# Score products of a differential attention: two low parts over 64 rows each instead of 128 rows padded with zeros

## The chip, the cores and the metric

The kernel runs on one core of one Trainium2 chip. The metric is the device time of one execution in microseconds; before the change it is 729.48 us, the median of three runs (729.27 to 730.88). All arithmetic is to float32 accuracy: a product that needs full accuracy is written as three products of "high" and "low" parts (the high part is the value rounded to the matrix engine's single-pass format, the low part is the rest).

## The reference, cut to what matters

Two layers over 512 positions of width 1024: a Mamba-2 layer (projections, a convolution, a chunked scan, an output projection) and a differential attention layer. The change is in the second. Eight heads each have two maps of 64 features; the scores of each map are softmaxed and the second map is subtracted with a weight:

```python
def attend_block(args):
    qb, blk = args
    ...
    scores = jnp.einsum("bhiqd,bhikd->bhiqk", qb, k).astype(jnp.float32) * scale
    scores = scores - slopes[None, :, None, None, None] * dist
    probs = jax.nn.softmax(jnp.where(allowed, scores, -jnp.inf), axis=-1)
    weights = probs[:, :, 0] - lam * probs[:, :, 1]
    return jnp.einsum("bhqk,bhke->bqhe", weights.astype(v.dtype), v)
```

## The kernel before, in words

TensorE runs a long dense stream of projections (z, g, o for the first layer; v, k, q, t for values, keys, queries and gates, then b and c for the output projection). Between pieces of it, small steps are put in at places that the program counts out: `beside(n)` lets the dense stream advance by n units (a 512-column triple of products is 2 of them), then the next small step is written. In the attention layer TensorE's instructions keep exactly the order in which they are written; VectorE's (DVE) and ScalarE's (ACT) are placed by a scheduler that works from a modelled timeline. Weights are fetched by DMA from SyncE into `raw`, split by ACT (`whi`) and DVE (`wlo`) one piece at a time, and used one stage later.

The small steps of a head h go over four tiles t of 128 queries. `scores(h, t)` makes the scores of both maps of that tile against the first n = (t + 1) * 128 keys; `weigh` and `turn` combine the two maps and transpose the result, `values` multiplies with v, `norm_head` and `gate_head` finish the head. A call of `scores` thus has products of 128, 256, 384 or 512 columns, eight calls of each width, 32 in all. The very last one, head 7 and tile 3, stands near the end, where the final projection (pc) runs out.

How a score is made: feature f of map m sits on partitions 64m to 64m + 63. The tile k2 (`two` in `feat_proj`) has for map m the high part of k on m's own 64 partitions and the low part on the other 64; q2 has the high part of q on both. One product over all 128 rows is therefore q_high times (k_high + k_low). The second product adds q_low times k_high: `q_lo` has, for map m, the low part of q on m's own 64 partitions and zeros on the other 64, so that k's low part is multiplied by nothing. These zeros are written once, by four memsets on GpSimd (POOL, line 897); DVE writes the low parts of each head into the other half (`q_lo<-pq,q` in the profile).

The products of one call stand in the order map 0 high, map 0 low, map 1 high, map 1 low, each pair into a bank of PSUM of its own (`ss_bank`, shown as sc). DVE then takes each map's bank with one instruction that scales, adds the distance penalty and finds the minimum (in the profile CUSTOM_DVE_ANT_0 s<-sc,bias), and ACT makes the exponentials and their sum (ACTIVATE s<-s,mx). The banks go round: three of the kind ss, and every fourth take is one of the four of the dense stream.

One other place uses part of the array: pyd in the scan of the first layer, whose products have 64 output columns and alternate between the upper and the lower half of the output partitions.

Nearly all instructions come through one helper, so the profile shows them at line 55; they are told apart by the tiles they write and read. PE is TensorE's products, PEld its loads of the stationary operand.

Of the kernel before, what the change touches and what calls it, by code (L numbers as in the profile page):

```python
# [9 lines left out]
F32 = mybir.dt.float32  # L10
F32R = mybir.dt.float32r
# [6 lines left out]
P = 128  # L18
S = 512
# [44 lines left out]
def trunk(ctx, tc, x, x_t, par, w_dt, w_in, w_out, w_kvqg, w_bo, d_skip, lam_qk, fin_g, out):  # L64
    nc = tc.nc
    V, A, T = (Ordered(tc, e) for e in (nc.vector, nc.scalar, nc.tensor))
    GP = nc.gpsimd
# [7 lines left out]
    def mm_bank(name):  # L75
        return psum.tile([P, 512], F32, tag="mm", name=name, bufs=4)
# [4 lines left out]
    def ss_bank(name):  # L81
        turns[0] += 1
        tag = "mm" if turns[0] % turns[1] >= 3 else "ss"
        return psum.tile([P, 512], F32, tag=tag, name=name, bufs=3 if tag == "ss" else 4)

    def long_bank(name):
        return psum.tile([P, 512], F32, tag="long", name=name)
# [118 lines left out]
    def use_b(seg, first=None, pace=None):  # L206
        i = segs.index(seg)
        while pieces:
            lay(pieces.pop(0))
        if i + 2 < len(segs) and fetched[0] == i + 2:  # L210
            loaded[i + 2] = load(i + 2)
        if seg == ("o", 3, 0):
            for piece in loaded.pop(i + 2)():
                lay(piece)
        if i + 1 in loaded:
            new = loaded.pop(i + 1)()
            pace = pace or 32 // len(new)
            pieces.extend(p + (pace if k else first or pace,) for k, p in enumerate(new))
        return ready.pop(seg)
# [15 lines left out]
    def mm3(ps, lhs, rhs, first, last, **kw):  # L235
        (lh, ll), (rh, rl) = lhs, rhs
        T.matmul(ps, lhsT=lh, rhs=rh, start=first, stop=False, **kw)
        T.matmul(ps, lhsT=lh, rhs=rl, start=False, stop=False, **kw)
        T.matmul(ps, lhsT=ll, rhs=rh, start=False, stop=last, **kw)
# [191 lines left out]
    q2 = sm.tile([P, P], F32, name="q2")  # L431
# [281 lines left out]
    cp = ctx.enter_context(tc.tile_pool(name="cp", bufs=1))  # L713
# [12 lines left out]
                yield 1  # L726
            A.copy(v_sb[:, t, cs], pv[:, 0:256])

    q_lo = [cp.tile([P, 2, S], F32R, name=f"q_lo{i}") for i in range(2)]
    kT, qT, gT, oT = {}, {}, {}, {}  # L730

    def feat_proj(pair):
        wh, wl = use_b((pair[0], pair, 0))
        for i in range(2):
            kind, h = pair[2 * i], int(pair[2 * i + 1])
            pf = mm_bank(f"p{kind}{h}")
            cs = slice(i * P, (i + 1) * P)
            for k in range(KD):
                mm3(pf, (wh[:, k, cs], wl[:, k, cs]), (hh[:, k, :], hl[:, k, :]), k == 0, k == KD - 1)
                yield 2  # L740
            if kind == "t":

                th = small.tile([P, S], F32, tag="wide", name=f"th{h}", bufs=2)
                A.activation(th, pf, AF.Tanh, scale=0.5)
                gt = cp2.tile([P, S], F32, tag="gt", name=f"gt{h}", bufs=3)
                V.scalar_tensor_tensor(out=gt, in0=th, scalar=1.0, in1=pf, op0=ALU.add, op1=ALU.mult)
                gT[h] = gt
            else:

                two = cp2.tile([P, 2, S], F32R, tag=f"{kind}2", name=f"{kind}2_{h}", bufs=4 if kind == "k" else 2)  # L750
                for m in range(2):
                    own, far = slice(64 * m, 64 * m + 64), slice(64 - 64 * m, 128 - 64 * m)
                    A.copy(two[own, m, :], pf[own, :])
                    if kind == "q":
                        A.copy(two[far, m, :], pf[own, :])
                    V.tensor_tensor(out=two[far, m, :] if kind == "k" else q_lo[h % 2][own, m, :], in0=pf[own, :],
                                    in1=two[own, m, :].bitcast(F32), op=ALU.subtract)
                (kT if kind == "k" else qT)[h] = two
            done.add(f"{kind}{h}")
# [18 lines left out]
    def stream_b():  # L778
        for it in ORDER_B:
            if it[0] == "c":  # L780
                yield from rows()
                return
            yield from b_out(int(it[1])) if it[0] == "b" else v_proj(int(it[1])) if it[0] == "v" else feat_proj(it)
            done.add(it)
# [3 lines left out]
    def scores(h, t):  # L788

        if t == 0:  # L790
            bias = cp2.tile([P, S], F32, tag="bias", name=f"bias{h}")
            V.tensor_scalar(out=bias, in0=dist, scalar1=-(2.0 ** (2 - h)), scalar2=None, op0=ALU.mult)
            st[h] = (bias, small.tile([P, 2, NT], F32, tag="mx", name=f"mx{h}"),
                     small.tile([P, 2, NT], F32, tag="sums", name=f"sums{h}"), [],
                     small.tile([P, NT], F32, tag="ratio", name=f"ratio{h}"), long_bank(f"po{h}"), [],
                     cp2.tile([P, NT, P], F32, tag="on", name=f"on{h}", bufs=2),
                     small.tile([P, NT], F32, tag="o_ss", name=f"o_ss{h}"))
        bias, mx, sums, s = st[h][0:4]
        k2, q2, ql = kT[h], qT[h], q_lo[h % 2]
        n = (t + 1) * P  # L800
        tq = slice(t * P, (t + 1) * P)
        s.append([cp2.tile([P, S], F32, tag=f"s{i}", name=f"s{h}_{t}_{i}", bufs=2) for i in range(2)])
        for i in range(2):
            ps = ss_bank(f"sc{h}_{t}_{i}")
            T.matmul(ps[:, :n], lhsT=q2[:, i, tq], rhs=k2[:, i, :n], start=True, stop=False)
            T.matmul(ps[:, :n], lhsT=ql[:, i, tq], rhs=k2[:, i, :n], start=False, stop=True)
            so = s[t][i][:, :n]
            V.tensor_tensor_reduce(out=so, in0=ps[:, :n], in1=bias[:, S - n:], scale=-0.125, scalar=3e38,
                                   op0=ALU.add, op1=ALU.min, accum_out=mx[:, i, t:t + 1])
            A.activation(so, so, AF.Exp, scale=-1.0, bias=mx[:, i, t:t + 1], accum_out=sums[:, i, t:t + 1])  # L810
# [81 lines left out]
    V.tensor_copy(dist, disti)  # L892
    A.activation(dist, dist, AF.Abs)
    GP.memset(dist[0:64, S - 64:S], BIG)
    for i in range(2):
        for m in range(2):
            GP.memset(q_lo[i][64 - 64 * m:128 - 64 * m, m, :].bitcast(F32), 0.0)
    lq = cp2.tile([P, 4, 64], F32, tag="gt", name="lq", bufs=3)
    nc.sync.dma_start(lq.rearrange("p a d -> p (a d)"), lam_qk.rearrange("a d -> (a d)").partition_broadcast(P))
    lqv = lq.rearrange("p (a b) d -> p a b d", b=2)  # L900
# [38 lines left out]
    def half(t, n):  # L939
        hs = slice(n * 512, (n + 1) * 512)  # L940
        return x_tok[:, t, hs], fg[:, hs], ot[t][:, hs], out[t * P:(t + 1) * P, hs]
# [40 lines left out]
    for h in range(DH):  # L982
        for t in range(NT):
            share = (13.0, 15.3, 17.6, 19.35)[t]
            if (h, t) == (DH - 1, 2):
                break
            scores(h, t)
            beside(share / 3)
            if h > 1 and t == 0:
                gate_head(h - 2)  # L990
            if last:
                turn(*last)
            beside(share * 2 / 3)
            if last:
                values(*last)
                if t == 0:
                    norm_head(h - 1)
            last = h, t


    h = DH - 1
    turns[:] = [0, 1]
    fg = res.tile([P, D], F32, tag="hT_lo", name="fg")
    nc.sync.dma_start(fg[:], fin_g.partition_broadcast(P))
    scores(h, 2)
    beside(6)
    gate_head(h - 1)
# [3 lines left out]
    norm_head(h, 0, 2)  # L1011
    beside(7.6)
    scores(h, 3)
    ot += [cp2.tile([P, D], F32, tag="k2", name=f"ot{t}", bufs=4) for t in range(NT)]
    beside(2)
# [45 lines left out]
    y, f, o, dst = half(3, 0)  # L1061
# [71 lines left out]
```

## Time and profile before

| | |
|---|---|
| median of three runs | 729.48 us (729.27 to 730.88) |
| profiled execution, its own time | 729.15 us |
| its span, first to last instruction | 727.0 us |
| busy TensorE products / loads | 713.5 / 593.1 us |
| busy VectorE / ScalarE / GpSimd | 528.0 / 433.7 / 117.7 us |
| TensorE share of the chain that ended last | 90% |
| first and last score product begin | 478.8 / 701.9 us |
| score products with q's high part, x64 | 223 to 481 ns each in the record |
| score products with q's low part, x64 | 273 to 398 ns each in the record |

A product's recorded duration runs from its issue to the modelled end of its results; neighbours overlap. What a product costs TensorE is read from the distance between the starts of neighbours. A row of the timeline gives start, duration (of all that were merged into it), engine, line, operation, output<-inputs, shape, and how many instructions. In a product's shape the first part is rows * columns of the array, the second the moving operand. A row of the chain of waits gives start, duration, engine, tile, and how many pieces were merged.

### The profile page before, as it was taken

Reading aid. Unit: us, or ns where it says so; the run is one execution under the profiler, and the core shown is the slowest. Engines: PE = TensorE matmul, PEld = TensorE weight load, DVE = VectorE, ACT = ScalarE, POOL = GpSimd, SP = SyncE. Lnnn points to the kernel's source line nnn. Section 1 sums busy time; section 2 is a strip of 40 time slices with the busy share of each in tenths; the row PEclk is TensorE's granted clock in tenths of the full one; section 3 lists DMA queues with packets and bytes.
Section 4 is the critical chain, followed back from the end, with each engine's and each line's share of the span. In section 5 each row is a group of like instructions: output and inputs, shape, how many; then the busy total and the mean of one; then the engine's idle time right before and its main releaser. Section 6 shows DMA issues by size and latency. Waiting matters only on the chain.

```text
span 727.0 us, 10819 instructions
## 1 busy us (share of the span) xinstructions
PE 713.5 (98%) x3989; PEld 593.1 (82%) x3989; DVE 528.0 (73%) x1202; ACT 433.7 (60%) x965; POOL 117.7 (16%) x158
## 2 busy tenths in 40 slices
PE   9999999999999999999999999999999999999996
PEld 7787888888888888887788869888988898889874
DVE  4688964979479668569995846657667857785886
ACT  5948573654735527527534348667766756756566
POOL 0108241412315024150110101000000000000002
PEclk9999999999999999999999999999999999999999
DMA  8634313314133231231122310331221131122003
GB/s 302 233 131 162 116 59 117 117 58 175 58 117 116 95 137 60 91 142 59 59 70 105 116 59 9 117 115 59 94 82 58 59 117 59 59 90 85 29 1 115
DMA packets 12916, 70.86 MB, mean 97 GB/s; under 512 B 1728, under 2 KB 2496, under 8 KB 5312
## 3 DMA queue, kind: packets, MB, share of 16 engines
q1 hardware_dynamic: 12576, 69.90, 26.5%
q8 instruction: 31, 0.51, 0.3%
q10 hardware_dynamic: 288, 0.28, 0.1%
q14 instruction: 21, 0.17, 0.1%
HBM read 68.02 MB, written 2.16 MB: 97 GB/s over the span
## 4 chain that ended last, share of the span: by engine, by line
PE 90%; DVE 7%; ACT 1%; issue 1%; POOL 0%; ACTq 0%; DVEq 0%; POOLq 0%
PE pg L55 21%; PE po L55 14%; PE pz L55 12%; PE pt L55 7%; PE pv L55 6%; PE pq L55 6%; PE pk L55 6%; PE pb L55 3%; PE sc L55 3%; PE pyd L55 2%; PE pc L55 2%; DVE wlo L55 2%; DVE xc L55 2%; PE pyt L55 1%; PE pxt L55 1%; PE psA L55 1%
## 5 line engine op out<-in xcount | busy, mean ns | idle before, releaser
L55 DVE SCALAR_TENSOR_TENSOR wlo<-raw,prm,whi 128x512 fp32r<-128x512 f32 (+1 forms) x256 | 150.4, 633 | 52.7 <-ACT whi L55 51.3
L55 ACT ACTIVATE whi<-raw,prm 128x512 fp32r<-128x512 f32 (+1 forms) x256 | 136.8, 606 | 81.4 <-PE pg L55 30.1
L55 PE MATMUL pg<-a_hi,whi 128*128 128x512 f32 x256 | 103.3, 404 | 1.5 <-DVE y_c L55 1.5
L55 PE MATMUL pg<-a_hi,wlo 128*128 128x512 f32 x256 | 102.3, 402 | 0.0
L55 PE MATMUL pg<-a_lo,whi 128*128 128x512 f32 x256 | 102.3, 400 | 0.0
L55 DVE SCALAR_TENSOR_TENSOR xc<-pg,prc,xc 128x511 f32<-128x511 f32 (+2 forms) x96 | 69.6, 738 | 4.8 <-ACT xc L55 4.4
L55 PEld LDWEIGHTS pg<-a_hi,whi 128*128 128x128 f32 x256 | 48.1, 188 | 13.1 <-issue 1.9
L55 PEld LDWEIGHTS pg<-a_hi,wlo 128*128 128x128 f32 x256 | 48.1, 188 | 11.0
L55 PEld LDWEIGHTS pg<-a_lo,whi 128*128 128x128 f32 x256 | 48.1, 188 | 10.7
L55 PE MATMUL po<-whi,yh 128*128 128x512 f32 x128 | 51.4, 402 | 1.5 <-DVE xc L55 0.8
L55 PE MATMUL po<-wlo,yh 128*128 128x512 f32 x128 | 51.1, 399 | 0.0
L55 PE MATMUL po<-whi,yl 128*128 128x512 f32 x128 | 50.4, 398 | 0.0
L55 PE MATMUL pz<-wlo,a_hi 128*128 128x512 f32 x128 | 50.3, 399 | 0.0
L55 PE MATMUL pz<-whi,a_lo 128*128 128x512 f32 x128 | 49.8, 398 | 0.0
L55 PE MATMUL pz<-whi,a_hi 128*128 128x512 f32 x128 | 49.6, 401 | 0.0
L971 POOL TENSOR_TENSOR ot<-ot,fg 128x512 f32<-128x512 f32 x4 | 5.1, 1289 | 256.9 <-ACT ot L55 256.9
L55 ACT ACTIVATE s<-s,mx 128x128 f32<-128x128 f32 (+3 forms) x64 | 35.5, 556 | 9.6 <-DVE mx L55 9.1
L55 ACT ACTIVATE xc<-pg,prc 128x512 f32<-128x512 f32 x32 | 24.6, 773 | 26.6 <-DVE pg L55 26.5
L589 POOL TENSOR_TENSOR xe<-xdt,tok 128x256 f32<-128x256 f32 x24 | 17.3, 749 | 139.6 <-DVE xdt L55 139.6
L55 DVE CUSTOM_DVE_ANT_0 s<-sc,bias 128x128 f32<-128x128 f32 (+3 forms) x64 | 29.4, 488 | 12.2 <-PE sc L55 11.7
L55 ACT ACTIVATE xc<-xc 128x512 f32<-128x512 f32 x32 | 20.0, 629 | 28.3 <-DVE xc L55 28.2
L55 PE MATMUL pv<-whi,b_hi 128*128 128x256 f32 x128 | 36.6, 286 | 0.0
(243 smaller groups left out, 1719.7 us busy)
## 6 DMA issues: line engine op xcount, KB each, us to landing
raw<-in_w_in SPq DMA_DIRECT2D x23, 1024.0 KB, 4.8
raw<-in_w_kvqg SPq DMA_DIRECT2D x16, 1024.0 KB, 4.8
dec<-acs_d SPq DMA_DIRECT2D x8, 1024.0 KB, 4.8
raw<-in_w_out SPq DMA_DIRECT2D x8, 1024.0 KB, 4.8
raw<-in_w_bo SPq DMA_DIRECT2D x4, 1024.0 KB, 4.8
x_tok<-in_x SPq DMA_DIRECT2D x4, 512.0 KB, 9.3
out<-ot SPq DMA_DIRECT2D x7, 256.0 KB, 2.4
raw<-in_w_in SPq DMA_DIRECT2D x4, 256.0 KB, 5.8
```

The costliest lines, as they stand in the source:

```text
L55: i = op(*args, **kw)
L589: GP.tensor_tensor(out=xe[:, c], in0=xdt[:, c], in1=toe_tok[:, c, hs].unsqueeze(2).to_broadcast([P, R, HD]), op=ALU.mult)
L971: GP.tensor_tensor(out=o, in0=o, in1=f, op=ALU.mult)
```

## The change

The low parts' tile is half as large and without zeros, the four memsets are gone, and the low products read only the map's own 64 partitions of both operands. Both banks of a call are taken first; the order of the four products is now map 0 high, map 1 high, map 0 low, map 1 low. What DVE and ACT do per map is the same.

```diff
-    q_lo = [cp.tile([P, 2, S], F32R, name=f"q_lo{i}") for i in range(2)]
+    q_lo = [cp.tile([P, S], F32R, name=f"q_lo{i}") for i in range(2)]
...
-                    V.tensor_tensor(out=two[far, m, :] if kind == "k" else q_lo[h % 2][own, m, :], in0=pf[own, :],
+                    V.tensor_tensor(out=two[far, m, :] if kind == "k" else q_lo[h % 2][own], in0=pf[own, :],
                                     in1=two[own, m, :].bitcast(F32), op=ALU.subtract)
...
+        pss = [ss_bank(f"sc{h}_{t}_{i}") for i in range(2)]
         for i in range(2):
-            ps = ss_bank(f"sc{h}_{t}_{i}")
-            T.matmul(ps[:, :n], lhsT=q2[:, i, tq], rhs=k2[:, i, :n], start=True, stop=False)
-            T.matmul(ps[:, :n], lhsT=ql[:, i, tq], rhs=k2[:, i, :n], start=False, stop=True)
+            T.matmul(pss[i][:, :n], lhsT=q2[:, i, tq], rhs=k2[:, i, :n], start=True, stop=False)
+
+        for i in range(2):
+            own = slice(64 * i, 64 * i + 64)
+            T.matmul(pss[i][:, :n], lhsT=ql[own, tq], rhs=k2[own, i, :n], start=False, stop=True)
+        for i in range(2):
+            ps = pss[i]
             so = s[t][i][:, :n]
...
-    for i in range(2):
-        for m in range(2):
-            GP.memset(q_lo[i][64 - 64 * m:128 - 64 * m, m, :].bitcast(F32), 0.0)
```

TensorE at the score call of head 0, tile 1, before. The name sc_1_0 is tile 1, map 0; the numbers at the ends of names are those of allocations and differ between the two programs by a constant.

```order
L55 MATMUL pq_4313<-b_hi,wlo_4231 128x512
L55 MATMUL sc_1_0_4368<-k_0_4185,q_0_4265 128x256
L55 MATMUL sc_1_0_4368<-k_0_4185,q_lo_3959 128x256
L55 MATMUL sc_1_1_4373<-k_0_4185,q_0_4265 128x256
L55 MATMUL sc_1_1_4373<-k_0_4185,q_lo_3959 128x256
L55 MATMUL pt_4385<-b_hi,whi_4230 128x512
```

The same place after the change:

```order
L55 MATMUL pq_4309<-b_hi,wlo_4227 128x512
L55 MATMUL sc_1_0_4364<-k_0_4181,q_0_4261 128x256
L55 MATMUL sc_1_1_4365<-k_0_4181,q_0_4261 128x256
L55 MATMUL sc_1_0_4364<-k_0_4181,q_lo_3959 128x256
L55 MATMUL sc_1_1_4365<-k_0_4181,q_lo_3959 128x256
L55 MATMUL pt_4381<-b_hi,whi_4226 128x512
```

Map 0's low product went behind map 1's high one; its neighbours of the dense stream are the same. All 32 calls on TensorE change in this way, the last one included, and nothing else on TensorE moves.

On DVE and ACT the scheduler moved a few rows by a place or two, on DVE in seven places, on ACT in three. DVE at a score call of tile 0, two heads' work side by side, before:

```order
L55 SCALAR_TENSOR_TENSOR wlo_4895<-raw_4734,prm,whi_4894 128x256 x5
L55 ISA s_0_0_4922,mx_4916<-sc_0_0_4924,bias_4914 128x128
L55 ISA mx_4916 128x1
L55 SCALAR_TENSOR_TENSOR wlo_4895<-raw_4734,prm,whi_4894 128x256
L55 ISA s_0_1_4923,mx_4916<-sc_0_1_4929,bias_4914 128x128
```

And after the change:

```order
L55 SCALAR_TENSOR_TENSOR wlo_4891<-raw_4730,prm,whi_4890 128x256 x6
L55 ISA s_0_0_4918,mx_4912<-sc_0_0_4920,bias_4910 128x128
L55 ISA mx_4912 128x1
L55 ISA s_0_1_4919,mx_4912<-sc_0_1_4921,bias_4910 128x128
L55 ISA mx_4912 128x1
```

The sixth piece of the weights' low part, which stood between the two maps' reductions, now stands ahead of both.

## The prediction

> **What bounds the kernel now.** First the page: its busy times and the chain that ended last.
>
> ```profile
> span 727.0 us, 10819 instructions
> PE 713.5 (98%) x3989; PEld 593.1 (82%) x3989; DVE 528.0 (73%) x1202; ACT 433.7 (60%) x965; POOL 117.7 (16%) x158
> PE 90%; DVE 7%; ACT 1%; issue 1%; POOL 0%; ACTq 0%; DVEq 0%; POOLq 0%
> ```
>
> TensorE sets the end: 90% of the chain is PE. A busy PE need not be a full one, so I next cut the span to the stretch that the change touches, from the first score product to just before the last call (478.6 to 701.3 us), and asked for the chain and the busy times there.
>
> ```profile
> by line: PE pt L55 21.2%; PE pq L55 17.6%; PE pv L55 15.1%; PE pk L55 15.1%; PE pb L55 9.9%; PE sc L55 8.6%; PE po L55 7.3%; PE pc L55 4.0%; PE pot L55 1.4%
> 478.60:701.30 222.70, 222.70 (x1274) 193.34 (x1273) 163.44 (x495) 147.21 (x423) 0.00 (x0) 1.00 0.20 69
> ```
>
> The chain is PE alone (the shares add up to all of it), PE is busy through all 222.70 us at the full clock (1.00), while DVE works 163.44 and ACT 147.21. So whatever TensorE gains or loses in 31 of the 32 score calls goes straight to the end. The pieces of that chain named sc give the price of one call, four products, for each of its widths of 128, 256, 384 and 512 keys; head 0's calls stand for the eight heads (the eight widest pieces are 0.92 or 0.93, save the last call's).
>
> ```profile
> 478.96 0.39 PE sc L55 x4
> 484.30 0.48 PE sc L55 x4
> 490.70 0.70 PE sc L55 x4
> 497.63 0.92 PE sc L55 x4
> ```
>
> A fourth of each is what one product takes of TensorE: 0.10, 0.12, 0.175 and 0.23 us.
>
> **What the change takes away.** Each call's two low products leave the full array and use 64 rows each, map 0 rows 0 to 63, map 1 rows 64 to 127, directly behind each other. The trace has no product over 64 rows; the nearest it has are the pyd products of the scan, which use 64 columns of the array, alternately the lower and the upper half.
>
> ```profile
> L55 PEld LDWEIGHTS pyd<-xdt,dec x512: 132/138/138, 78.2 to 408.3; 128*64 128x64 f32 x171
> L55 PE MATMUL pyd<-xdt,dec x512: 222/222/270, 78.2 to 408.4; 128*64 128x64 f32 x171
> ```
>
> ```profile
> 406.90 0.40 PE L55 MATMUL po<-whi,yh 128*128 128x512 f32 x1
> 407.14 0.39 PE L55 MATMUL po<-wlo,yh 128*128 128x512 f32 x1
> 407.46 0.28 PE L55 MATMUL pyd<-xdt,dec 128*64 128x64 f32 x2
> 407.46 0.14 PEld L55 LDWEIGHTS pyd<-xdt,dec 128*64 128x64 f32 x2 [0.37 <-issue]
> ```
>
> Two products of up to 270 ns each are over in 0.28 us, their two loads of at least 132 ns in 0.14: the halves work at the same time, about 0.01 us apart. If row halves do the same, each call pays one low product instead of two. Saved: 8 x (0.10 + 0.12 + 0.175 + 0.23) = 5.0 us. The bounds are 0 (the pair runs one after the other) and 5.0; I take 5.0, because two halves of the same array is the nearest row.
>
> **What the change adds.** The same rows show a price. From one full 512-column product to the next is 0.24 us (406.90 to 407.14; 0.23 in the sc rows), but the load for the half array begins 0.32 after the last full product (407.14 to 407.46), and it waits for nothing that the profile shows ("issue"). So 0.09 us pass between the end of the full stream and the load. Elsewhere a load begins with the product ahead of it (last two rows below) and costs nothing. An earlier entry and two exits, the other way:
>
> ```profile
> 84.09 0.40 PE L55 MATMUL pg<-a_hi,wlo 128*128 128x512 f32 x1
> 84.42 0.31 PEld L55 LDWEIGHTS pyd<-xdt,dec 128*64 128x64 f32 x8 [0.37 <-DVE xc L55]
> ...
> 78.93 0.46 PE L55 MATMUL pyd<-xdt,dec 128*64 128x64 f32 x10
> 79.32 0.19 PEld L55 LDWEIGHTS pg<-a_hi,whi 128*128 128x128 f32 x1
> 79.33 0.50 PE L55 MATMUL pg<-a_hi,whi 128*128 128x512 f32 x1
> 79.66 0.40 PE L55 MATMUL pg<-a_lo,whi 128*128 128x512 f32 x1
> ...
> 403.39 0.46 PE L55 MATMUL pyd<-xdt,dec 128*64 128x64 f32 x10
> 403.78 0.19 PEld L55 LDWEIGHTS po<-whi,yl 128*128 128x128 f32 x1
> 403.78 0.50 PE L55 MATMUL po<-whi,yl 128*128 128x512 f32 x1
> 404.12 0.39 PE L55 MATMUL po<-whi,yh 128*128 128x512 f32 x1
> 404.12 0.19 PEld L55 LDWEIGHTS po<-wlo,yh 128*128 128x128 f32 x1
> ```
>
> The entry at 84 us has the same 0.33, though there a semaphore is named, so the semaphore is not what it waits for. At the exit at 403 us the last half product begins at 403.39 + 0.46 - 0.22 = 403.63. Five pairs begin within the 0.24 us before that, 0.06 apart, so the next product was due at 403.69. Its load begins at 403.78, again 0.09 late, and its row reads 0.50 instead of 0.40: it sits 0.10 waiting for its weights, and the stream behind it is regular again only from 404.12 - 0.23 = 403.89. Late by 0.20 us. The exit at 79 us gives the same (79.66 - 0.23 = 79.43 against 79.17 + 0.06). So a switch of the array's division costs 0.09 of emptying and, with 128 columns of weights, 0.10 of a load that lies open: 0.19 us. The load of pyd is half as wide; the low products load 128 columns, so they pay the 0.10 of the exit rows on the way in too.
>
> [...]
>
> Before, each low product followed a full one with nothing between. Now a call goes: two full products, switch, the pair, switch. For 256 keys and more: in 0.19, out 0.19, and 0.01 to 0.02 for the pair's second start, 0.40 in all. For 128 keys the stream is short (a fourth of 0.23, so 0.06) and the 0.10 that such a product takes today is the load's: in 0.06 + 0.09 + 0.10 - 0.11 = 0.14, out the same and 0.01, together 0.29. Sum: 24 x 0.40 + 8 x 0.29 = 11.9 us. Bounds per switch: nothing (rows are free) and 0.20 (the largest that the exits show). I take the trace's 0.19.
>
> **The sum** for PE: 11.9 - 5.0 = +6.9 us.
>
> The last call has no such cover behind it; there the chain leaves PE:
>
> ```profile
> 701.25 0.39 PE L55 MATMUL sc<-k,q 128*128 128x512 f32 x1
> 701.47 0.39 PE L55 MATMUL sc<-k,q_lo 128*128 128x512 f32 x1
> 701.70 0.39 PE L55 MATMUL sc<-k,q 128*128 128x512 f32 x1
> 701.92 0.39 PE L55 MATMUL sc<-k,q_lo 128*128 128x512 f32 x1
> 701.90 0.69 DVE L55 CUSTOM_DVE_ANT_0 s<-sc,bias 128x512 f32<-128x512 f32 x1
> 702.51 0.69 DVE L55 CUSTOM_DVE_ANT_0 s<-sc,bias 128x512 f32<-128x512 f32 x1
> ```
>
> ```profile
> 701.90 0.69 DVE s L55
> 702.63 1.53 ACT s L55 x4
> 704.60 0.64 DVE pc L55
> 705.24 0.33 DVE ol L55
> 705.62 1.19 PE pc L55 x4
> ```
>
> DVE takes map 0 as soon as its low product (the second) is through, at 701.90. Now that product comes third and behind the switch: one further full product and 0.19, so map 0 is ready about 0.43 us later, while map 1 is ready at about the same time. PE itself is late by 0.40 - 0.23 = 0.17 in this call; the chain through DVE and ACT by 0.43, so 0.26 more. Total +7.2: span 734.2. The profiled execution takes 729.15 with a span of 727.0, so 2.15 lie around it: 736.35. The median of the runs is 0.33 over that execution: **736.6 us**, say 736.5.
>
> **What costs nothing.** Four memsets go from POOL:
>
> ```profile
> L897 POOL MEMSET q_lo<- x4: 520/520/522, 443.0 to 444.7; 64x512 f32 x4
> ```
>
> They end at 445, 33 us before the first score product, and POOL has no work in the stretch above. The 31 earlier calls give DVE map 0 late by up to 0.43 us, 13 us together; queued behind that reduction on DVE are the wlo parts of weights that PE needs one stage on, and ACT's exponentials. DVE has 222.70 - 163.44 = 59 us free, so PE should not notice; were the cover gone, up to 13 us more. The few wlo rows that change places with a reduction lie in the same cover. The second map's bank is wanted one product earlier (0.10 to 0.23 us); its reader three takes before is at least a transpose and its copy, microseconds back, so nothing.
>
> **Rivals.**
>
> *Row halves switch for nothing* (faster). One mechanism, at the two borders of each call: if loads for 64 rows go in behind a running full product as other loads do, the 11.9 us vanish and the 5.0 stay: 722.0 span, 724.5 us. It decides from a switch under 5.0 / 64 = 0.08 us on. For it: all 16 entries to and exits from pyd are column switches, so the trace says nothing of rows. Against it: the 0.09 comes before the load, both in and out, behind pg as behind po, which looks like emptying the array and not like something that column halves alone need. [...]
>
> *Emptying but no open load*: the switch costs 0.09 for the wide calls and 0.045 for the narrow (0.06 + 0.09 - 0.11). 24 x 0.20 + 8 x 0.10 = 5.6 against 5.0, +0.6; with half products that neither overlap nor switch it would be 0. About 730. For: loads elsewhere go early. Against: the 0.50 of both exits.
>
> *The pair doesn't overlap*: both start and accumulate into banks of their own, but if the second waits for the first, the 5.0 are lost and the switches stay: 741.6. Against: the 0.28 for two pyd products.
>
> **How the numbers follow.** Forecast 0.59, with a range of its own: emptying 0.06 to 0.12 and a load of 0.08 to 0.12 make +3.5 to +10, 733 to 739.5. Free switches 0.19 (724.5), half price or no effect 0.14 (about 730), no overlap 0.08 (741.6). The range, 728 to 742, leaves out the free switches. What a measurement of this kernel can tell from no change is about 0.2%, 1.5 us: faster 0.19; same 0.12 (most of the half price, the rest falls above); slower 0.69.
>
> **What would show it.** In the changed profile, in each call: the load of the first low product begins about 0.09 after the end of the second full stream instead of with its start; the two low rows begin about 0.01 apart; the product behind them reads some 0.10 longer than its kind; from the first score product of a 512-key call to the product behind it about 1.10 us instead of 0.93, of a 128-key call 0.65 instead of 0.45. PE would still be busy through the stretch, which would be 6.5 to 7 us longer. Wrong would be: low loads that begin with the second full product (free switches), low rows a whole product apart (no overlap), or idle time on PE named after DVE wlo (the cover of DVE was thinner than I say).

## The result and the profile after

| | before | after |
|---|---|---|
| median of the runs beside each other | 729.94 us (729.27 to 730.88) | 738.28 us (737.42 to 738.83) |
| profiled execution: its span | 727.0 us | 736.0 us |
| first score product | 478.80 us | 480.72 us |
| first product of the last score call | 701.25 us | 709.79 us |
| from the one to the other, 31 calls | 222.45 us | 229.07 us |
| from there to the end | 25.77 us | 26.18 us |

The two first score products, before and after (the row of the last call before, 701.25, stands in the prediction, the one after, 709.79, below):

```profile
478.80 0.22 PE L55 MATMUL sc<-k,q 128*128 128x128 f32 x1
480.72 0.22 PE L55 MATMUL sc<-k,q 128*128 128x128 f32 x1
```

The change makes the kernel slower: ratio 1.0116, interval 1.0103 to 1.0129, or 8.3 us. The page after:

```profile
span 736.0 us, 10813 instructions
PE 721.2 (98%) x3989; PEld 589.7 (80%) x3989; DVE 529.0 (72%) x1202; ACT 433.4 (59%) x965; POOL 117.2 (16%) x154
PE 90%; DVE 7%; ACT 1%; issue 1%; POOL 0%; ACTq 0%; DVEq 0%; POOLq 0%
```

TensorE still sets the end, with as many products. The chain and the busy times of the stretch from the first score product to the last call:

```profile
by line: PE pt L55 21.2%; PE pq L55 17.5%; PE pv L55 15.3%; PE pk L55 15.2%; PE pb L55 10.0%; PE sc L55 8.7%; PE po L55 7.1%; PE pc L55 3.9%; PE pot L55 1.3%
480.70:709.75 229.05, 229.05 (x1272) 189.96 (x1271) 163.21 (x494) 147.09 (x422) 0.00 (x0) 1.00 0.19 67
```

The chain is again PE alone, DVE and ACT have the same work as before (163 and 147 us), and the clock is full: 6.6 us more, all of them TensorE's. One call of 512 keys in the timeline shows where (a row that says x2 begins with the first and lasts to the end of the second):

```profile
499.99 0.30 PEld L55 LDWEIGHTS sc<-k,q 128*128 128x128 f32 x2
500.02 0.71 PE L55 MATMUL sc<-k,q 128*128 128x512 f32 x2
500.66 0.19 PEld L55 LDWEIGHTS sc<-k,q_lo 64*128 64x128 f32 x2 [0.37 <-issue]
500.66 0.49 PE L55 MATMUL sc<-k,q_lo 64*128 64x512 f32 x2
501.08 0.19 PEld L55 LDWEIGHTS pk<-b_hi,whi 128*128 128x128 f32 x1 [0.24 <-issue]
501.09 0.50 PE L55 MATMUL pk<-b_hi,whi 128*128 128x512 f32 x1
501.43 0.39 PE L55 MATMUL pk<-b_lo,whi 128*128 128x512 f32 x1
```

The two loads for 64 rows are over in the time of one (0.19), and so are the two low products (0.49): the halves work together. But the loads begin 0.32 us after the start of the second full product, which begins at 500.02 + 0.71 - 0.39 = 500.34, instead of with its start (before, pk's load and the product ahead of it both began at 498.16), and wait for nothing that the profile shows. On the way out the load for pk begins 0.42 after the pair. By the author's estimate 0.10 of this is the pair's wait for its own load (its row reads 0.49, where the full low product of the last call before reads 0.39), 0.23 its stream and 0.09 the wait behind it; pk's first product reads 0.50, not 0.40 as before, and its neighbour follows after 0.34 instead of 0.24. From the first score product to where the stream is regular again (501.43 - 0.23 = 501.20) it is 1.18 us. Before, the same call took 1.00:

```profile
497.39 0.47 PE L55 MATMUL sc<-k,q 128*128 128x512 f32 x1
498.39 0.40 PE L55 MATMUL pk<-b_hi,whi 128*128 128x512 f32 x1
498.63 0.39 PE L55 MATMUL pk<-b_lo,whi 128*128 128x512 f32 x1
```

And at the end of the program, the last call and what VectorE makes of it:

```profile
709.79 0.61 PE L55 MATMUL sc<-k,q 128*128 128x512 f32 x2
710.34 0.50 PE L55 MATMUL sc<-k,q_lo 64*128 64x512 f32 x2
710.88 0.69 DVE L55 CUSTOM_DVE_ANT_0 s<-sc,bias 128x512 f32<-128x512 f32 x1 [0.48 <-PE sc L55]
711.49 0.69 DVE L55 CUSTOM_DVE_ANT_0 s<-sc,bias 128x512 f32<-128x512 f32 x1
```

DVE begins map 0 1.09 us after the call's first product; before it was 701.90 - 701.25 = 0.65. That is 0.44 later, and the time from the last call to the end grew by 0.41.

So the score stretch and the end give 6.62 + 0.41 = 7.0 of the span's 9.0 us. The other 1.9 lie ahead of the first score product, in work that is the same in both kernels. There the granted clock (the column behind ACT's and POOL's busy times) tells most of it:

```profile
328.50:332.50 4.00, 2.11 (x10) 1.43 (x9) 4.00 (x11) 3.95 (x4) 0.00 (x0) 1.00 0.00 0
332.50:335.90 3.40, 3.40 (x10) 2.65 (x9) 2.31 (x5) 3.39 (x5) 0.00 (x0) 0.50 0.00 0
335.90:339.30 3.40, 3.40 (x16) 2.72 (x16) 3.40 (x6) 3.40 (x9) 0.00 (x0) 1.00 0.00 0
```

For 3.4 us TensorE ran at half clock and began 10 products where 16 fit in: 6 x 0.23 = 1.4 us. In the profile before, the same place kept the full clock (17 products):

```profile
328.00:332.00 4.00, 2.47 (x11) 1.75 (x10) 4.00 (x11) 3.95 (x4) 0.21 (x1) 1.00 0.00 0
332.00:335.40 3.40, 3.40 (x17) 2.72 (x16) 2.31 (x5) 3.39 (x5) 0.00 (x0) 1.00 0.00 0
```

### The profile page after: what moved, and what is told of

It is laid out like the page before. It is cut to its first block, busy times and chain, and to the rows that moved or that the text cites. A ratio compares the mean times of both kernels' runs of the same rounds, so it can differ in the third digit from the quotient of the medians.

```text
span 736.0 us, 10813 instructions
## 1 busy us (share of the span) xinstructions
PE 721.2 (98%) x3989; PEld 589.7 (80%) x3989; DVE 529.0 (72%) x1202; ACT 433.4 (59%) x965; POOL 117.2 (16%) x154
## 4 chain that ended last, share of the span: by engine, by line
PE 90%; DVE 7%; ACT 1%; issue 1%; POOL 0%; ACTq 0%; DVEq 0%; POOLq 0%
PE pg L55 21%; PE po L55 14%; PE pz L55 12%; PE pt L55 7%; PE pv L55 6%; PE pq L55 6%; PE pk L55 6%; PE pb L55 3%; PE sc L55 3%; PE pyd L55 2%; DVE wlo L55 2%; PE pc L55 2%; DVE xc L55 2%; PE pyt L55 1%; PE pxt L55 1%; PE psA L55 1%
## 5 line engine op out<-in xcount | busy, mean ns | idle before, releaser
L55 DVE SCALAR_TENSOR_TENSOR wlo<-raw,prm,whi 128x512 fp32r<-128x512 f32 (+1 forms) x256 | 152.5, 642 | 52.9 <-ACT whi L55 51.7
```

The lines of the kernel that those rows point to most:

```text
L55: i = op(*args, **kw)
```

## The experiments

The theory: each division of the array into row halves, and each return from it, costs TensorE 0.09 of emptying and 0.10 of an open load, and the overlap of the pair pays only part of it. (The rows show the 0.09 as a wait between the end of the stream and the next load; what the array does in it they don't show, and "emptying" is a name for it.) Rivals: the new order (VectorE gets map 0 later), products over 64 rows that are slow in themselves, a pair that doesn't overlap. In each run below the stretch runs from the first score product to the first of the last call, two rows of its timeline, and its median stands beside that of the kernel before on the same chip.

### The order alone

```diff
-            T.matmul(pss[i][:, :n], lhsT=ql[own, tq], rhs=k2[own, i, :n], start=False, stop=True)
+            T.matmul(pss[i][:, :n], lhsT=ql[:, i, tq], rhs=k2[:, i, :n], start=False, stop=True)
```

with `q_lo` and its zeros as before.

> The kernel before, with its low products over all 128 rows and with their zeros, but in the new order (map 0 high, map 1 high, map 0 low, map 1 low) and both banks taken first. Switch theory (the loss comes from dividing the array into row halves and undoing it): no switch, so TensorE's stretch is as long as before; only the last call's map 0 is ready one product later, +0.2 us: 730.1 against 729.9 before. Rival, the order (VectorE gets map 0 later in every call, and its cover is thin): +7 to +8, about 738, as the changed kernel.

Measured: 732.11 us (12 runs) against 730.9 (17 runs), ratio 1.001, interval 0.9992 to 1.0028.

```profile
481.03 0.22 PE L55 MATMUL sc<-k,q 128*128 128x128 f32 x1
703.52 0.39 PE L55 MATMUL sc<-k,q 128*128 128x512 f32 x1
```

The stretch is 222.49 us, before 222.45; from the last call to the end it is 26.02 instead of 25.77, the 0.25 of map 0 behind one more product. In the stretch the order costs 0.04 us: VectorE's cover holds. The interval ends 2.0 us above the kernel before, so this rival, +7 to +8, falls.

### Two visits in each call

```diff
         for i in range(2):
-            T.matmul(pss[i][:, :n], lhsT=q2[:, i, tq], rhs=k2[:, i, :n], start=True, stop=False)
-        for i in range(2):
+            ps = ss_bank(f"sc{h}_{t}_{i}")
             own = slice(64 * i, 64 * i + 64)
-            T.matmul(pss[i][:, :n], lhsT=ql[own, tq], rhs=k2[own, i, :n], start=False, stop=True)
+            T.matmul(ps[:, :n], lhsT=q2[:, i, tq], rhs=k2[:, i, :n], start=True, stop=False)
+            T.matmul(ps[:, :n], lhsT=ql[own, tq], rhs=k2[own, i, :n], start=False, stop=True)
```

> The changed kernel's 64-row low products, but each directly behind its own map's high product, as in the order before: the array is divided and undone twice in each call, and the two halves never work together. Switch theory: each visit costs 0.19 in and 0.19 out for 256 keys and more, 0.14 and 0.14 for 128, and nothing is saved: 24 x 0.76 + 8 x 0.56 = +22.7 against before, 752.6 us. Rival, the order: as before, 730. Rival, products over 64 rows are slow in themselves and switching is free: as the changed kernel, 738, or 5 more.

Measured: 753.69 us against 730.9, ratio 1.0312, interval 1.0284 to 1.0341.

```profile
479.29 0.22 PE L55 MATMUL sc<-k,q 128*128 128x128 f32 x1
500.04 0.48 PE L55 MATMUL sc<-k,q 128*128 128x512 f32 x1
500.45 0.49 PE L55 MATMUL sc<-k,q_lo 64*128 64x512 f32 x1
500.87 0.50 PE L55 MATMUL sc<-k,q 128*128 128x512 f32 x1
501.31 0.49 PE L55 MATMUL sc<-k,q_lo 64*128 64x512 f32 x1
501.73 0.50 PE L55 MATMUL pk<-b_hi,whi 128*128 128x512 f32 x1
724.47 0.39 PE L55 MATMUL sc<-k,q 128*128 128x512 f32 x1
```

The stretch is 245.18 us, 22.7 over before; the forecast was 22.7 for 32 calls, 22 for these 31. Neighbours in the 512-key call begin 0.41 to 0.44 apart where a product needs 0.23: each crossing adds 0.18 to 0.21, forecast 0.19. Doubling the visits and dropping the overlap costs as the theory says, and the order rival and the slow-products rival (730 and 738 to 743) fall.

### The same half for both maps

```diff
-            own = slice(64 * i, 64 * i + 64)
+            own = slice(0, 64)
```

> The changed kernel with one edit: map 1's low product reads rows 0 to 63 as map 0's does (so it multiplies the wrong parts, and map 1's scores lack their low part). The switches stay, the overlap of the pair goes. If the pair overlaps in the changed kernel, each call pays a second low product: + 8 x (0.10 + 0.12 + 0.175 + 0.23) = +5.0 over the changed kernel, 743.3 us. If the pair doesn't overlap there, no change: 738.3.

Measured: 745.12 us (741.59 to 746.07) against 730.9, ratio 1.0181, interval 1.0151 to 1.0211. A call of 512 keys:

```profile
499.02 0.70 PE L55 MATMUL sc<-k,q 128*128 128x512 f32 x2
499.65 0.29 PEld L55 LDWEIGHTS sc<-k,q_lo 64*128 64x128 f32 x2 [0.35 <-issue]
499.65 0.73 PE L55 MATMUL sc<-k,q_lo 64*128 64x512 f32 x2
500.31 0.50 PE L55 MATMUL pk<-b_hi,whi 128*128 128x512 f32 x1
```

The two ends of the stretch:

```profile
479.35 0.22 PE L55 MATMUL sc<-k,q 128*128 128x128 f32 x1
713.29 0.39 PE L55 MATMUL sc<-k,q 128*128 128x512 f32 x1
```

Now the two low products take 0.73 instead of 0.49 and their loads 0.29 instead of 0.19: one behind the other. The stretch is 233.94, 4.9 over the changed kernel's. So the pair does overlap in the change, and in TensorE's stretch the overlap is worth what was forecast. The median is 14.2 us over the kernel before, more than the 11.9 that stretch and end give here; the last experiment comes back to such differences.

### The pair twice

```diff
-        for i in range(2):
-            own = slice(64 * i, 64 * i + 64)
-            T.matmul(pss[i][:, :n], lhsT=ql[own, tq], rhs=k2[own, i, :n], start=False, stop=True)
+        for z in range(2):
+            for i in range(2):
+                own = slice(64 * i, 64 * i + 64)
+                T.matmul(pss[i][:, :n], lhsT=ql[own, tq], rhs=k2[own, i, :n], start=False, stop=z == 1)
```

> The changed kernel with the pair of low products issued twice in each call (the low part counts double in the scores). Switch theory: the number of switches is the same, and inside the divided array a second pair costs as much as one product of the stream, its loads hidden: +5.0 over the changed kernel, 743.3 us. If the loads of the second pair lie open as those of the first do: 0.10 x 32 more, 746.5. If the price belongs to 64-row products and not to the switches: the whole loss and the saving once more, about +11.9, 750.

Measured: 743.33 us against 730.9, ratio 1.0168, interval 1.0139 to 1.0197. The same call:

```profile
499.05 0.71 PE L55 MATMUL sc<-k,q 128*128 128x512 f32 x2
499.69 0.30 PEld L55 LDWEIGHTS sc<-k,q_lo 64*128 64x128 f32 x4 [0.37 <-issue]
499.69 0.73 PE L55 MATMUL sc<-k,q_lo 64*128 64x512 f32 x4
500.36 0.50 PE L55 MATMUL pk<-b_hi,whi 128*128 128x512 f32 x1
```

The two ends of the stretch:

```profile
479.34 0.22 PE L55 MATMUL sc<-k,q 128*128 128x128 f32 x1
713.36 0.39 PE L55 MATMUL sc<-k,q 128*128 128x512 f32 x1
```

Four low products take 0.73, as two in one half did. The stretch is 234.02, 4.95 over the changed kernel's: a second pair costs 4.95 / 31 = 0.16 a call, as much as one product, and the four loads (0.30) lie within the 0.73. The price belongs to the crossing, not to 64-row products.

### No low products

```diff
-            T.matmul(pss[i][:, :n], lhsT=q2[:, i, tq], rhs=k2[:, i, :n], start=True, stop=False)
-
-        for i in range(2):
-            own = slice(64 * i, 64 * i + 64)
-            T.matmul(pss[i][:, :n], lhsT=ql[own, tq], rhs=k2[own, i, :n], start=False, stop=True)
+            T.matmul(pss[i][:, :n], lhsT=q2[:, i, tq], rhs=k2[:, i, :n], start=True, stop=True)
```

> The changed kernel without its low products (the scores lack q's low part): no switch, two full products a call. If a low product over the full array costs TensorE a fourth of a call's piece and all of it counts, this is 2 x 5.0 = 10.0 us under the kernel before, about 720, and 17 under the changed kernel. If part of the low products lay in time that TensorE had anyway, less than 10: for example 725 if half did.

Measured: 720.47 us against 729.95, ratio 0.9866, interval 0.9842 to 0.989.

```profile
479.52 0.22 PE L55 MATMUL sc<-k,q 128*128 128x128 f32 x1
692.30 0.39 PE L55 MATMUL sc<-k,q 128*128 128x512 f32 x1
```

The stretch is 212.78, 9.67 under before: two low products over the full array cost 0.31 a call, all of it on the path. This gives a price list per call, from stretches of 31 calls: a visit with one pair (229.07 - 212.78) / 31 = 0.53 us, a further pair 4.95 / 31 = 0.16, so the two crossings 0.37; two visits with one product each (245.18 - 212.78) / 31 = 1.05, twice 0.53. A visit with j pairs costs 0.37 + 0.16 j, the full array 0.31 j: the visit pays from 2.5 pairs on. By this estimate, a mean over the four widths, a visit for two query tiles would still lose 0.07.

The widths differ, though. The same differences between the runs, taken call by call (from the start of the second product ahead of a call to the start of the fourth behind it, mean over the calls of a width without the very last):

| columns | two low products, full array | visit with one pair | each further pair | so both crossings | pays from |
|---|---|---|---|---|---|
| 128 | 0.22 us | 0.40 us | 0.12 us | 0.28 us | 2.7 pairs |
| 256 | 0.24 us | 0.51 us | 0.12 us | 0.39 us | 3.4 pairs |
| 384 | 0.35 us | 0.57 us | 0.18 us | 0.40 us | 2.3 pairs |
| 512 | 0.46 us | 0.62 us | 0.24 us | 0.39 us | 1.8 pairs |

At 512 columns a visit with two pairs would by this estimate already gain 0.05 us. No run tried visits that serve two query tiles, or three pairs or more: each pair that waits there holds two banks beside those of the dense stream.

### The changed kernel again

> The changed kernel once more, beside more runs of the kernel before on the same chip. In its first profile the stretch of the score calls and the end were 7.0 us longer than before, while the runs differed by 8.3 and the span by 9.0; the other 1.9 of the span lie ahead of the first score product, where both kernels are alike, and 3.4 us of that stretch ran at half the granted clock. If that half-clock stretch falls into executions of either kernel at random, the runs here differ by 7.0 to 7.5 us and the score stretch is again 6.6 us longer. If the change brings it about, they differ by 8.3 or more and the profile shows the half-clock stretch again near 332 us.

Measured: 738.37 us (735.96 to 741.15, 6 runs) against 729.95 (11 runs), ratio 1.0113, interval 1.0092 to 1.0135, that is 6.7 to 9.9 us. This time no half-clock stretch fell into the profiled execution, at 332 us or elsewhere before the end:

```profile
core 0: 733.9 us, clock 0.998
478.59 0.22 PE L55 MATMUL sc<-k,q 128*128 128x128 f32 x1
707.67 0.39 PE L55 MATMUL sc<-k,q 128*128 128x512 f32 x1
```

The score stretch is 229.08 once more, and the span is 6.8 over before instead of 9.0. So the changed kernel doesn't always meet the half clock at 332 us. Two other runs met one at another place, the order alone, which never divides the array for the scores, and the same half for both maps (half clock, the 0.50, from 424.9 and 422.9 us on):

```profile
420.90:424.90 4.00, 2.71 (x13) 1.38 (x12) 1.06 (x5) 2.78 (x6) 0.00 (x0) 1.00 0.72 262
424.90:428.30 3.40, 3.40 (x10) 2.62 (x9) 0.81 (x2) 0.00 (x0) 0.00 (x0) 0.50 0.00 0
```

```profile
418.90:422.90 4.00, 2.70 (x13) 1.36 (x12) 1.01 (x6) 2.52 (x6) 0.00 (x0) 1.00 0.66 262
422.90:426.30 3.40, 3.40 (x9) 2.62 (x10) 1.09 (x2) 0.26 (x1) 0.00 (x0) 0.50 0.00 0
```

But the medians still differ by 8.4, not 7.0 to 7.5. This interval holds 7.0, the first result's (7.5 to 9.4) does not. Where some 1.3 us of the timed difference come from was not settled. More half-clock stretches in the changed kernel are not what the recorded clocks say: one such stretch lowers the mean clock of an execution by 0.5 x 3.4 / 734 = 0.0023, and the six executions here have a mean clock of 0.9977, the eleven of the kernel before 0.9974. To make up 1.3 us, about one stretch more (some 1.4 us) would be needed in each execution. The timed differences stray from the traces elsewhere too: in the other experiments the difference of the medians lies between 0.5 us under (two visits) and 2.3 us over (the same half) what stretch and end give, and ahead of the first score product the eight profiled executions differ by up to 2.4 us (478.59 to 481.03).

## Why the prediction was right

By its own steps:

- **What bounds.** PE alone in the score stretch: right, before and after, and the order alone left the stretch at 222.49 us (before 222.45). DVE's 59 us of cover held.
- **Saved, 5.0 us.** Right: taking the overlap away cost 4.9, and all low products together cost 9.7 (forecast from the chain's pieces 10.0 for 32 calls, 9.5 for these 31).
- **Added, 0.19 per crossing.** Right in size and in both its parts: in the 512-key call the low loads begin 0.32 after the start of the last full product, 0.09 after its stream of 0.23 ends, and the first product on the way out reads 0.50 instead of 0.40. That row halves pay what column halves pay was the author's estimate: the trace before has no product over 64 rows, only pyd's two exits, each 0.20 late, 0.09 and 0.10 of it told by the rows. In the 512-key call of the two visits row halves cost 0.18 to 0.21 a crossing.
- **The sum for PE.** 6.9 for 32 calls, 6.7 for the 31 of the stretch; measured 6.6. It is right term by term, not by errors that cancel: calls of 128, 256, 384 and 512 keys grew by 0.18, 0.28, 0.22 and 0.17 us (measured as in the table by width), and the forecast's terms give 0.19, 0.28, 0.225 and 0.17.
- **The end.** Map 0 0.43 later; measured 0.44, and 0.41 at the end. The +7.2 in all was 7.0 in the traces.
- **The time.** 736.5 against 738.28: the remaining 1.8 is the 1.3 that the last experiment leaves open, and 0.5 by which the kernel before was slower beside it (729.94 for 729.48). The forecast's own addends, 736.35 and 0.33, make 736.7; it wrote 736.6 and took 736.5.
- **The rivals.** Switches for nothing: the two loads at 500.66, 0.32 after the start of the product ahead of them, rule it out. Emptying without an open load: the 0.50 of pk, where 0.40 is usual, rules it out. No overlap: 0.49 for two products rules it out.

One sign named in the prediction was put inexactly: from the first product of a 512-key call "to the product behind it" 1.10 instead of 0.93. The rows give 1.07 instead of 1.00 there, because the open load on the way out falls behind the start of that product; measured to the regular stream it is 1.18 instead of 1.00, about the 0.17 that the sum had. In both kernels this is 0.07 to 0.08 more than forecast, since the call's first product itself takes longer (0.32 from 500.02 to 500.34, where 0.23 is usual). For a 128-key call the forecast's 0.65 instead of 0.45 also holds only to the regular stream: 0.63 instead of 0.45 at head 0, while the product behind the call begins after 0.52 instead of 0.40. The two low products of a pair begin 0.003 to 0.004 us apart, forecast about 0.01.

## What to carry to other kernels

Before products are moved to part of TensorE's array, price the crossings: here a visit cost 0.37 us on average for going in and out, with one product, one pair or two pairs inside, and each pair of half-array products inside cost 0.16 instead of the 0.31 of the full array. By these numbers a visit must carry several such pairs (2.5 on average; about 2 at 512 columns, 3 to 4 at 256) or it is cheaper to leave zeros in the full array. If the kernel already divides the array anywhere, look at the rows around that place for the price: here the 0.19 read from the column halves of pyd held for the row halves (0.18 to 0.21 a crossing in the two visits).

## What the runs showed of the hardware that was not expected

Three profiled executions had a stretch of 3.4 us at half clock (0.50) behind 4 us in which TensorE waited for part of the time: in the changed kernel's first profile it followed 4 us with 2.11 us of work and cost about 1.4 us; in the order alone and in the same half for both maps it followed 4 us with 2.71 and 2.70 us of work. Another profiled execution of the changed kernel had none before the end, and the kernel before none either, though they had only 2.46 and 2.47 us of work in the 4 us ahead of the first of these places. So the amount of work in the 4 us ahead does not sort these cases, and the runs don't show what does.
